# Ordering one kernel's instructions with the scheduler's other machine model

## The chip, the cores and the metric

The kernel is one program on one NeuronCore of a Trainium2 chip. The metric is the time of one execution on the device in microseconds (us). Five engines run side by side, each through its own fixed list of instructions: TensorE (PE; its weight loads are shown apart, as PEld), VectorE (DVE), ScalarE (ACT), GpSimd (POOL) and SyncE (SP), which issues most transfers. An instruction waits for the data that it reads and for the buffer that it writes, and what stands behind it on its engine waits with it.

## The reference

Two transformer-like blocks over 512 tokens of width 1024, batch 1, in float32. The first has an attention layer and a recurrent layer, the second two feed-forward parts around a mixer. Cut to what matters here:

```python
# first block, attention layer: neighbourhood attention (8 heads) and grouped-query attention
y = concat([o_a * silu(ga), o_b * silu(gb)]) @ w_out
# first block, recurrent layer: RWKV state scan in both directions, and a Hyena long convolution
s = s * w_t - sa * b_t + v_t * k_t;  y = s @ r_t           # RWKV, one token
kern = hyena_filters(512, ...)                             # taps, transformed to spectra
z = gate * fft_long_conv(z, kern[:, o], skip[o])           # Hyena, two orders
# second block, mixer: three branches, each with a gate
sol = triangular_solve(a_mat, rhs)                         # gated delta rule, chunks of 64
v_new = u_n - w_n @ state                                  # then 8 chunks in sequence
o = qd_n @ state + qk_n @ v_new
state = state * gl_n + kd_n.T @ v_new
gates = sigmoid(u @ w_branch_gate)                         # 1024 -> 3 x 1024
merged = gates[0] * (o_nsa @ w_nsa) + gates[1] * (o_dn @ w_dn) + gates[2] * (o_mem @ w_mem)
```

## The kernel before

`main()` writes out the whole computation for all five engines in program order, inside a `tile.TileContext`. Tiles come from pools with a number of buffers each, and the context's scheduler decides afterwards in which order the instructions of each engine stand: it plays the program through on a machine model, and at each step an engine takes, of the instructions that the model says could start, the one with the best priority. Priority is program order, moved by `tc.high_priority(...)`. No order is written by hand apart from that.

**Matrix products.** Each large product is split in float32r halves: `wblock` (L96 to L110) loads a weight block `wraw`, ScalarE rounds it to `whi` (L108), VectorE subtracts to get `wlo` (L109), and `mm3` issues three matmuls (L114 to L116): high by high, high by low, low by high. In the rows `mm<-lath,whi` is the input projection of the recurrent layer, `gt<-hh,whi` the gates and other mixer projections, `mm<-whi,oh` the attention layer's output projection. They wait for little but weights, so they can fill TensorE while something else waits.

**Chains.** Four stages have long chains of small steps that go from engine to engine:
- RWKV (`rwkv`, from 760 to 1290 us): six windows of chunks. `unit_inverse` (L1314) inverts triangular blocks: a stream transpose (L1321), 31 pairs of multiply and add on VectorE (L1331, L1333), two stream transposes (L1336, L1337), then 32 by 32 matmuls (L1351, L1353). The steps (`ru` tiles, L1368 to L1429) follow.
- Hyena's spectra (`hy_spectra`): taps (L1575), their squares summed (L1589), products with tables (`fx<-eh,tab0h` and the like), through the pool `fx` with one bank; beside it stands the grouped-query attention (L405, L439, L775).
- DeltaNet (`deltanet`, L2091): per 128 tokens transposes (L2131, L2166) and products (L2177, L2178); one inverse for all heads; then 8 chunks, each of them this loop:

```python
mm(R, T["kbe"], St)                       # L2200, TensorE
Rs = R + vb                               # L2204, VectorE
solve_T(U, TT, Rs)                        # L1368, TensorE
Vs = copy(U)                              # L2207, ScalarE
mm(Q, kd, Vs)                             # L2211, TensorE
St = Q + gl * St                          # L2219, VectorE (L2218 on GpSimd ahead of it)
mm(O, T["qe"], St_old); mm(O, QK, Vs)     # L2223, L2225, TensorE
```
- The mixer's tail: `dn_out` (transposes L2248 of the normalised DeltaNet output), `mem_attn`, `nsa` (L1988) and `merge` with matmuls of 128 columns.

Program order puts `mix_gates` behind `deltanet`, and `RecIn.rest` and `hy_conv` behind the RWKV steps, the last two with a priority part of the way up (`at(x)` in `rwkv`).

## Time and profile before

| | |
|---|---|
| time, median of 3 runs | 2866.03 us (2864.94 to 2867.31) |
| the profiled execution's own time | 2864.4 us |
| its span, first to last instruction | 2861.5 us |
| busy: PE / PEld / DVE / ACT / POOL | 2645.9 / 2125.4 / 1495.3 / 1028.4 / 503.8 us |
| mean granted clock of TensorE | 0.951 of full speed |

The profiled execution lies 1.6 us below the median, and its span 2.9 us below its own time. The granted clock has two levels, 1.0 (2.4 GHz) and 0.5 (1.2 GHz); a figure between them is a mean over a stretch. A pause of TensorE is told with the instruction that ends it and what released that instruction.

### The profile page before, as it was taken

How to read it: one execution, taken by the hardware profiler on the slowest of the kernel's cores; microseconds unless marked ns; L12 is line 12 of the kernel's file. 1: busy time of each engine (PE TensorE's matmuls, PEld its weight loads, DVE VectorE, ACT ScalarE, POOL GpSimd, SP SyncE). 2: the span in 40 equal slices, each digit the busy share in tenths (PEclk: the TensorE clock that was granted, in tenths of full speed). 3: DMA queues.
4: the chain of work that ended last, by engine and by line, in shares of the span. 5: the costliest groups of instructions: out<-in, count | busy, mean ns of one | idle time of the engine just before them, and what ended most of it. 6: DMA issues, size and time to landing. Idle time of an engine off the chain costs nothing.

```text
span 2861.5 us, 43340 instructions
## 1 busy us (share of the span) xinstructions
PE 2645.9 (92%) x16642; PEld 2125.4 (74%) x16642; DVE 1495.3 (52%) x3219; ACT 1028.4 (36%) x2165; POOL 503.8 (18%) x803
## 2 busy tenths in 40 slices
PE   8998998989989889878999998999989999899998
PEld 5897445678767666658888877777868776888887
DVE  4144557736487888685344237762232566444423
ACT  4223335524344444223333224432222663323322
POOL 1011001222343332432000001311010344100000
PEclk9999899989899899988999998999987999999999
DMA  6111431142223332524333323232453315233332
GB/s 231 60 60 55 145 119 63 57 129 81 83 87 113 90 93 66 174 94 138 96 96 96 96 85 108 83 96 91 122 160 104 106 55 161 89 100 100 96 96 88
DMA packets 251018, 290.60 MB, mean 102 GB/s; under 512 B 17415, under 2 KB 197082, under 8 KB 250812
## 3 DMA queue, kind: packets, MB, share of 16 engines
q1 hardware_dynamic: 239292, 251.29, 28.4%
q0 software_dynamic: 10704, 33.41, 3.9%
q8 instruction: 131, 2.15, 0.3%
q10 hardware_dynamic: 816, 3.15, 0.3%
q14 instruction: 75, 0.61, 0.1%
HBM read 247.38 MB, written 35.68 MB: 99 GB/s over the span
## 4 chain that ended last, share of the span: by engine, by line
PE 71%; DVE 11%; issue 5%; POOL 5%; DMA 4%; ACT 3%; SPq 0%; DVEq 0%; POOLq 0%; ACTq 0%
PE mm L114 13%; PE mm L115 13%; PE mm L116 13%; PE gt L114 3%; PE gt L115 3%; PE gt L116 3%; PE ac L116 1%; PE ac L115 1%; PE ac L114 1%; PE ac L874 1%; PE fx L333 1%; PE ac L2053 1%; PE mm L813 1%; DVE wlo L109 1%; PE tr L857 1%
## 5 line engine op out<-in xcount | busy, mean ns | idle before, releaser
L109 DVE TENSOR_TENSOR wlo<-wraw,whi 128x512 fp32r<-128x512 f32 (+1 forms) x390 | 374.5, 961 | 690.1 <-ACT whi L108 683.3
L108 ACT ACTIVATE whi<-wraw 128x512 fp32r<-128x512 f32 (+1 forms) x390 | 323.7, 831 | 792.5 <-PE mm L115 224.3
L114 PE MATMUL mm<-hh,whi 128*128 128x512 f32 (+1 forms) x1024 | 384.0, 376 | 1.0 <-ACT hh L178 0.7
L115 PE MATMUL mm<-hl,whi 128*128 128x512 f32 (+1 forms) x1024 | 383.5, 375 | 0.0
L116 PE MATMUL mm<-hh,wlo 128*128 128x512 f32 (+1 forms) x1024 | 383.0, 374 | 0.1
L114 PEld LDWEIGHTS mm<-hh,whi 128*128 128x128 f32 x1024 | 193.8, 190 | 35.7 <-ACT hh L178 1.3
L116 PEld LDWEIGHTS mm<-hh,wlo 128*128 128x128 f32 x1024 | 193.5, 189 | 35.2 <-DVE wlo L109 1.2
L115 PEld LDWEIGHTS mm<-hl,whi 128*128 128x128 f32 x1024 | 193.9, 189 | 33.1
L114 PE MATMUL mm<-whi,mh 128*128 128x512 f32 (+1 forms) x480 | 172.4, 360 | 1.4 <-DVE th L2270 1.4
L115 PE MATMUL mm<-wlo,mh 128*128 128x512 f32 (+1 forms) x480 | 173.0, 360 | 0.1
L116 PE MATMUL mm<-whi,ml 128*128 128x512 f32 (+1 forms) x480 | 172.7, 360 | 0.0
L114 PE MATMUL gt<-hh,whi 128*128 128x512 f32 (+1 forms) x320 | 128.7, 402 | 7.0 <-ACT whi L108 6.4
L116 PE MATMUL gt<-hh,wlo 128*128 128x512 f32 (+1 forms) x320 | 128.3, 401 | 0.8 <-DVE wlo L109 0.8
L115 PE MATMUL gt<-hl,whi 128*128 128x512 f32 (+1 forms) x320 | 127.6, 399 | 0.0
L283 POOL TENSOR_TENSOR ss<-sq 128x1 f32<-128x1 f32 x8 | 1.6, 201 | 707.3 <-ACT th L277 707.3
L114 PE MATMUL mm<-lath,whi 128*128 128x512 f32 (+1 forms) x280 | 116.4, 417 | 0.1
L116 PE MATMUL mm<-lath,wlo 128*128 128x512 f32 (+1 forms) x280 | 113.7, 407 | 1.0 <-DVE wlo L109 1.0
L115 PE MATMUL mm<-latl,whi 128*128 128x512 f32 (+1 forms) x280 | 113.3, 405 | 0.4 <-DVE latl L179 0.4
L114 PEld LDWEIGHTS mm<-whi,mh 128*128 128x128 f32 x480 | 89.9, 188 | 15.8 <-DVE th L2270 1.8
L115 PEld LDWEIGHTS mm<-wlo,mh 128*128 128x128 f32 x480 | 90.1, 188 | 14.4 <-DVE wlo L109 0.8
L116 PEld LDWEIGHTS mm<-whi,ml 128*128 128x128 f32 x480 | 90.1, 188 | 13.8
L114 PEld LDWEIGHTS gt<-hh,whi 128*128 128x128 f32 x320 | 62.2, 194 | 21.7 <-ACT whi L108 7.4
(732 smaller groups left out, 5987.7 us busy)
## 6 DMA issues: line engine op xcount, KB each, us to landing
wraw<-in_ffn_w_gate SPq DMA_DIRECT2D x44, 512.0 KB, 3.5
wraw<-in_ffn_w_up SPq DMA_DIRECT2D x44, 512.0 KB, 3.6
wraw<-in_ffn_w_down SPq DMA_DIRECT2D x44, 512.0 KB, 3.7
wraw<-in_w_in SPq DMA_DIRECT2D x60, 256.0 KB, 2.8
wraw<-in_rec_w_in SPq DMA_DIRECT2D x58, 256.0 KB, 2.8
wraw<-in_attn_w_in SPq DMA_DIRECT2D x26, 512.0 KB, 3.7
ada_w<-in_rec_ada_w SPq DMA_DIRECT2D x24, 512.0 KB, 3.7
wraw<-in_w_branch_gate SPq DMA_DIRECT2D x48, 256.0 KB, 3.0
```

Source lines behind the costliest of these rows:

```text
L108: nc.scalar.activation(hi, raw, AF.Copy)
L109: self.weng.tensor_sub(lo, raw, hi.bitcast(F32))
L114: mm(out, lh, rh, start=start, stop=False)
L115: mm(out, lh, rl, start=False, stop=False)
L116: mm(out, ll, rh, start=False, stop=stop)
L283: nc.gpsimd.tensor_add(ss, sq[:, i, 0:1], sq[:, i, 1:2])
L333: nc.tensor.matmul(p[o:o + 32], self.cs[:, kk], w[:, k], start=kk < 4, stop=kk >= 4, tile_position=(0, o))
L813: nc.tensor.matmul(ps[p][:, o:o + n], qaT[heads[p], pr, 128 * i:128 * i + 128], ks[p], start=True, stop=True)
L857: nc.tensor.transpose(t[:, j * 128:j * 128 + 128], s[:, a:a + 128], b.ident)
L874: nc.tensor.matmul(o[heads[p], xs], va[rows, n, h * 64:h * 64 + 64], pT[rows, p, j, xs], start=j == 0, stop=j == nk - 1)
L2053: nc.tensor.matmul(o, r["v"][br][:, j], pT[br][:, j].rearrange("p a b -> p (a b)"), start=False, stop=br == 1 and j == i)
```

## The change

One argument of the context is set. The scheduler then plays the program through on its other machine model, which keeps queues and engines in time. No instruction of the computation is added or taken away: TensorE has the same matmuls and DMA queues the same transfers. What differs is the order in which each engine has them, and with it the semaphore waits. TensorE's list has 15,558 lines of difference (10,856 rows before and 11,173 after, where like instructions in a row are one row), VectorE's 5,104.

```diff
-    with tile.TileContext(nc) as tc:
+    with tile.TileContext(nc, schedule_with_timeline_sim=True) as tc:
         main(tc, I, out[0])
```

TensorE at the start of DeltaNet's chunks, before (rows 7350 to 7361; `ac<-Rs,TT` is the solve, `pq<-Vs,kd` the state's product, `ac<-St,Tkbe` the next chunk's first product):

```order
L1368 MATMUL ac<-Rs,TT 64x128 x4
L114 MATMUL gt<-hh,whi 128x512
L115 MATMUL gt<-hl,whi 128x512
L116 MATMUL gt<-hh,wlo 128x512
L114 MATMUL gt<-hh,whi 128x512
L2211 MATMUL pq<-Vs,kd 128x128 x4
L115 MATMUL gt<-hl,whi 128x512
L116 MATMUL gt<-hh,wlo 128x512
L114 MATMUL gt<-hh,whi 128x512
L115 MATMUL gt<-hl,whi 128x512
L2225 MATMUL pq<-Vs,QK 64x128 x4
L2200 MATMUL ac<-St,Tkbe 64x128 x4
```

The same place after the change (rows 7523 to 7533; L2131 is the last transpose of the preparation, L1351 and L1353 the inverse's matmuls):

```order
L2131 MATMUL tr<-ident,dn_16378 128x128
L1351 MATMUL tr<-inv_n,NT 32x32 x32
L1353 MATMUL tr<-TT,inv_x 32x32 x32
L1368 MATMUL ac<-Rs,TT 64x128 x4
L2211 MATMUL pq<-Vs,kd 128x128 x4
L2225 MATMUL pq<-Vs,QK 64x128 x4
L2200 MATMUL ac<-St,Tkbe 64x128 x4
L1368 MATMUL ac<-Rs,TT 64x128 x4
L2211 MATMUL pq<-Vs,kd 128x128 x4
L2223 MATMUL pq<-St,Tqe 64x128 x4
L2225 MATMUL pq<-Vs,QK 64x128 x4
```

Before, some four gate matmuls stand between any two steps of the chain, and 109 rows of them between the last preparation (row 7227) and L1351 (row 7337). After, none stands from the last preparation (row 7523) to row 7562, behind the eighth chunk; the gates' rows stand ahead of it, among the preparation, or from row 7563 on.

TensorE at the fifth of RWKV's six inverses, before (rows 4001 to 4012; `iv` and `mm_10818` are RWKV's own, `mm<-lath` and `mm<-latl` the input projection):

```order
L1351 MATMUL iv<-inv_n,N 32x32 x32
L1198 MATMUL mm_10818<-KR_10792,kT_10795 128x128 x2
L115 MATMUL mm<-latl,whi 128x512
L116 MATMUL mm<-lath,wlo 128x512
L114 MATMUL mm<-lath,whi 128x512
L115 MATMUL mm<-latl,whi 128x512
L116 MATMUL mm<-lath,wlo 128x512
L1353 MATMUL iv<-TT,inv_x 32x32 x32
L1153 MATMUL mm_10846<-lora,wu 128x128 x4
L114 MATMUL mm<-lath,whi 128x512
L115 MATMUL mm<-latl,whi 128x512
L116 MATMUL mm<-lath,wlo 128x512
```

The same inverse after the change (rows 4077 to 4088; L1153 to L1259 are RWKV's preparation of the next window, L1387 the first matmul of a step):

```order
L1198 MATMUL mm_10818<-KR_10792,kT_10795 128x128 x8
L1153 MATMUL mm_10846<-lora,wu 128x128 x4
L1153 MATMUL mm_10878<-lora,wu 128x128 x4
L1351 MATMUL iv<-inv_n,N 32x32 x32
L1219 MATMUL tr<-ident,kT_10870 128x128 x4
L1198 MATMUL mm_10905<-KR_10867,kT_10870 128x128 x8
L1353 MATMUL iv<-TT,inv_x 32x32 x32
L1219 MATMUL tr<-ident,kT_10902 128x128 x4
L1198 MATMUL mm_10925<-KR_10899,kT_10902 128x128 x8
L1259 MATMUL iv<-ident,vw 64x128 x4
L1257 MATMUL iv<-ident,vpad 128x128 x4
L1387 MATMUL ru<-VU_10945,AK 64x64
```

Behind the fourth inverse 208 matmuls of the input projection stand before the change and 9 after it; behind the fifth, 122 before and none after. The rest have moved ahead of it. A third place, in words: behind the last matmul of grouped-query attention (L775) stand no matmuls of Hyena's spectra before the change, and 100 matmul rows after it, a whole last group with L1575 and L1589.

The two feed-forward parts keep their order on TensorE.

## Rows read from the trace of the kernel before

**Rows 1.** The page: span; busy time of each engine; the chain that ended last.
```profile
span 2861.5 us, 43340 instructions
...
PE 2645.9 (92%) x16642; PEld 2125.4 (74%) x16642; DVE 1495.3 (52%) x3219; ACT 1028.4 (36%) x2165; POOL 503.8 (18%) x803
...
PE 71%; DVE 11%; issue 5%; POOL 5%; DMA 4%; ACT 3%; SPq 0%; DVEq 0%; POOLq 0%; ACTq 0%
```

**Rows 2.** Busy time by stretch: from:to length, PE PEld DVE ACT POOL, PEclk, DMA share, GB/s.
```profile
440.00:600.00 160.00, 140.86 (x851) 100.32 (x850) 111.33 (x257) 89.54 (x207) 29.84 (x38) 0.95 0.18 59
760.00:1000.00 240.00, 211.43 (x1931) 165.01 (x1932) 184.39 (x444) 104.77 (x231) 89.42 (x153) 0.88 0.33 96
1000.00:1200.00 200.00, 175.47 (x2189) 131.49 (x2188) 153.31 (x386) 77.67 (x178) 69.20 (x110) 0.97 0.36 112
1330.00:1710.00 380.00, 371.14 (x1759) 311.94 (x1758) 146.81 (x166) 111.68 (x150) 8.72 (x22) 0.99 0.29 90
1800.00:2040.00 240.00, 228.33 (x1396) 176.39 (x1394) 115.76 (x225) 79.92 (x141) 42.95 (x55) 0.99 0.32 96
1920.00:1960.00 40.00, 40.00 (x337) 29.81 (x329) 12.40 (x18) 12.38 (x21) 8.39 (x10) 1.00 0.18 56
2060.00:2200.00 140.00, 122.22 (x582) 105.42 (x581) 38.68 (x68) 26.49 (x51) 16.08 (x27) 0.76 0.47 128
```

**Rows 3.** Groups on VectorE from 1894 to 1919.6: line, operation | busy us, mean ns | idle before.
```profile
L1333 DVE TENSOR_TENSOR inv_x<-inv_x,inv_t 128x126 f32<-128x126 f32 (+22 forms) x31 | 7.9, 256 | 0.9
L1331 DVE TENSOR_TENSOR inv_t<-inv_n,inv_x 128x126 f32<-128x126 f32 (+22 forms) x31 | 7.9, 255 | 0.9
L109 DVE TENSOR_TENSOR wlo<-wraw,whi 128x512 fp32r<-128x512 f32 x9 | 6.1, 682 | 0.0
L1321 DVE STREAM_TRANSPOSE inv_n<-NT 128x1024 f32<-128x1024 f32 x1 | 2.0, 2019 | 0.0
...
L1336 DVE STREAM_TRANSPOSE inv_n<-inv_x 128x512 f32<-128x512 f32 x1 | 1.1, 1061 | 0.0
```

**Rows 4.** Timeline of one DeltaNet chunk: start us, us, engine, line, operation [idle <- releaser].
```profile
1930.13 1.09 PE L2200 MATMUL ac<-St,Tkbe 128*64 128x128 f32 x8
...
1931.26 0.69 DVE L2204 TENSOR_TENSOR Rs<-ac,vb 64x512 f32<-64x512 f32 x1 [2.47 <-PE ac L2200]
...
1932.27 1.08 PE L1368 MATMUL ac<-Rs,TT 64*64 64x128 f32 x8
...
1933.39 0.59 ACT L2207 ACTIVATE Vs<-ac 64x512 f32<-64x512 f32 x1 [2.56 <-PE ac L1368]
...
1934.40 1.16 PE L2211 MATMUL pq<-Vs,kd 64*128 64x128 f32 x8
...
1935.66 0.69 DVE L2219 TENSOR_TENSOR St<-pq,Sg 128x512 f32<-128x512 f32 x1 [0.27 <-PE pq L2211]
...
1936.62 1.09 PE L2223 MATMUL pq<-St,Tqe 128*64 128x128 f32 x8
...
1938.65 1.09 PE L2200 MATMUL ac<-St,Tkbe 128*64 128x128 f32 x8
```

**Rows 5.** TensorE's timeline behind a pause of 12 us.
```profile
1724.53 1.76 PE L166 MATMUL tr<-ident,x 128*128 128x128 f32 x7 [12.02 <-DVE x L157]
```

**Rows 6.** Busy time by stretch behind that pause; columns as in rows 2.
```profile
1730.00:1732.00 2.00, 2.00 (x11) 2.00 (x10) 1.55 (x3) 0.74 (x2) 0.00 (x0) 0.50 0.12 18
1734.00:1736.00 2.00, 2.00 (x19) 1.88 (x19) 1.25 (x2) 1.20 (x2) 0.00 (x0) 1.00 0.00 0
```

**Rows 7.** TensorE's waits from 2060 to 2200: us in total, times, longest.
```profile
PE pq L2248 <- DVE on L2245: 7.1, 3, 4.2
PE gt L114 <- ACT whi L108: 5.5, 1, 5.5
```

**Rows 8.** TensorE's timeline at 607 us.
```profile
607.57 0.80 PE L114 MATMUL mm<-whi,oh 128*128 128x256 f32 x2 [9.13 <-ACT whi L108]
```

**Rows 9.** Line 1589: count, ns min/median/max, first and last start us.
```profile
L1589 PE MATMUL fx<-ones,sq x32: 250/250/370, 480.9 to 577.1; 128*128 128x1 f32 x32
```

## The prediction

> **What bounds the kernel now.** I read the page first: TensorE is busy 2645.9 of 2861.5 us, and the chain that ended last runs through TensorE for 71% of the span [rows 1]. The change takes no work away, so only the other 2861.5 − 2645.9 = 215.6 us can move, together with the matmuls that run at the half clock and are therefore longer. The second view is the table of busy time by stretch [rows 2], to see where those 215.6 us lie. In the first feed-forward stretch (1330 to 1710) TensorE is busy 371.1 of 380 us; its order stays, so nothing changes there. The rest is in four stages:
> - attention beside Hyena's spectra, 440 to 600: 160 − 140.9 = 19.1 us idle, and a pause of 9.13 us behind it [rows 8];
> - RWKV, 760 to 1000: 240 − 211.4 = 28.6 idle, with a mean clock of 0.88; 1000 to 1200: 24.5 idle, with VectorE busy 153.3 of 200;
> - DeltaNet, 1800 to 2040: only 240 − 228.3 = 11.7 idle, and from 1920 to 1960, where its chain of chunks runs, none at all;
> - the mixer's tail, 2060 to 2200: 17.8 idle, at a mean clock of 0.76.
>
> The reader should see that DeltaNet is nearly free now. Its chain is as long as ever, but gate matmuls fill every hole of it. What the order does to that cover decides the forecast.
>
> **The change part by part.** Durations are measured, from the profiled execution before; where the instructions stand comes from the two orders. Nothing here is a time out of the scheduler's own model.
>
> *DeltaNet's inverse.* Before, 109 rows of gate matmuls lie between the last preparation and L1351; afterwards none. What TensorE will then wait for is VectorE's chain: 7.9 + 7.9 us for the 31 pairs, 1.8 idle between them, 2.0 and 1.1 for the stream transposes, 20.7 in all [rows 3]. The nine L109 subtractions that are woven in before (6.1 us) are not counted, since the gates' weights move with the gates. To this come the masking of the last products ahead of it, and a copy behind each of L1351 and L1353; with each such step at the 0.6 to 0.7 us of the copies in [rows 4], and six of them, this is 4. The inverse costs **+25** of idle TensorE.
>
> *DeltaNet's chunks.* Before, a chunk takes 1938.65 − 1930.13 = 8.52 us, and TensorE never stops [rows 4]. Laid bare, the loop is L2200 1.09, Rs 0.04 + 0.69, solve 1.08, Vs 0.04 + 0.59, L2211 1.16, St 0.10 + 0.69, then L2223 and L2225 from 1936.62 to 1938.65, 2.03: together 7.51 us, of which TensorE idles 0.73 + 0.63 + 0.79 = 2.15. Eight chunks make **+17**. The chunk gets shorter, by a microsecond, but the three microseconds of gate matmuls that it carried are now elsewhere, and take time there.
>
> Against these stands the idle time of 1800 to 2040 that is there now, 11.7. Denser gates ahead of the chain can remove most of it; I credit **−8**. DeltaNet nets +34. Its bounds: +42 with nothing credited; and +16, if half of the holes of inverse and chunks (21) is hidden by something that I don't see and 5 of the 11.7 is credited.
>
> *The clock behind the bare stretch.* A pause of 12.02 us is in the trace [rows 5]. Some 6 us after it, TensorE is full but does 11 matmuls in 2 us at a granted clock of 0.50; at 1734 it does 19 at 1.00 [rows 6]. A pause of 25 us ends in the same way, and the work behind it here is the chunk loop, where TensorE has 7.51 − 2.15 = 5.36 us of work in 7.51. I take **+6**: the first chunk or so at half clock, 5.36 each. Lower bound 0; upper bound all eight chunks, 8 × 5.36 = 43.
>
> The Trainium skill, in "TensorE: Matmul & The Clock Gate", section "HAM oscillation — how this bites in real kernels", says that a loop whose matmul bursts alternate with waits can be throttled again at each wait and so stay slow. Here the row shows a single recovery after one pause, and no row shows such a loop at either clock; by the row the sum has +6, by the page it would have up to +43. This is the third rival below.
>
> *RWKV.* The input projection is used up early: 208 of its matmuls stand behind the fourth inverse before, 9 after; behind the fifth 122 and none. One takes about 371.1 / 1759 = 0.21 us (the mean of the feed-forward stretch [rows 2], whose matmuls are of the same kind). So 122 × 0.21 = 26 us of cover is missing where the last two inverses and the steps run, and 199 × 0.21 = 42 us stands earlier, where there are 28.6 us of idle time to fill. Both happen. If VectorE's chain is what the stage waits for throughout (it is busy 77% of it), the early filling gains nothing, because the fill then delays the steps, and the late holes cost. I take **+7**, between −42 (all of the moved work goes into idle time and slow clock, and the tail is set by VectorE anyway) and +26. It is nearer to the middle than to either end because the two amounts are of a size.
>
> *Spectra beside attention.* A whole last group of spectra now runs behind the last attention matmul. Between the four L1589 groups lie (577.1 − 480.9) / 3 = 32 us each, with attention woven in [rows 9]; alone a group has some 96 table matmuls, and if they run at half of the 0.21 us, since they have half of the columns, 10 us of work. Its holes are then at most 32 − 10 = 22. Against it, the 9.13 us pause, which waits for the first output weights [rows 8], can shrink behind a later start of that product, and attention without spectra has its part of the 19.1. I take **+5**, between −9 and +22.
>
> *The mixer's tail.* Here the order may help. Its 17.8 us of idle time contain 7.1 of L2248 waiting for VectorE and 5.5 of gates waiting for `whi` [rows 7]; afterwards L2248's transposes are spread among matmuls. The clock of 0.76 over 140 us means that about 0.24 / 0.5 × 140 = 67 us were at half; without the 17.8 idle, that is 49 us of work that would take 25 at full clock. At most 17.8 + 25 = 43 can be won, and at least nothing, since the same matmuls of 128 columns come again behind the same kind of waits. I take **−20**, half.
>
> The sum: 34 + 6 + 7 + 5 − 20 = +32. Made against the profiled execution, 2864.4 + 32 = 2896.4, whose own time lies 1.6 us below the median; the forecast is 2898 us. TensorE's weight loads, GpSimd and the DMA queues are put at nothing: the transfers are the same, and a dense run of fills asks for weights no faster than the feed-forward stretch, which keeps TensorE full with a DMA share of 0.29 [rows 2]. Without that cover the known price is one more pause like the 9.13 us [rows 8].
>
> **The rivals.**
> - *Faster: RWKV's early filling pays in full.* One mechanism: 42 us of input projection falls into the 28.6 us of idle time and the half clock of 760 to 1000 (0.88 means 0.12 / 0.5 × 240 = 58 us at half), and VectorE's chain is not delayed by it. Then the RWKV term is about −40 instead of +7, and the time 2898 − 47 = 2851; with a tail that wins its whole 43 as well, 2828. For it speaks that the idle time is really there; against it, that VectorE is busy 77% there and steps now stand behind fills in TensorE's list. It decides when the stage from 760 us gets shorter by more than 26 us plus what the tail wins less than 20.
> - *Nothing: the same.* All terms cancel and TensorE's 2645.9 us of work decide: 2866. For it: 92% busy. Against it: DeltaNet's 42 us of holes have no row that fills them.
> - *Much slower: the clock stays at half* through the chunk loop (+43 instead of +6) and the tail wins nothing: 2898 + 37 + 20 = 2955; with only the first, 2935. For it: the clock of 0.76 in the tail, where waits are shorter than the inverse. Against it: the recovery in [rows 6].
>
> **How the numbers follow.** A difference of 0.2% (5.7 us) is about what a measurement of this kernel can tell from none. Likeliest, the sum: 0.55, with its own range of 2878 to 2922. The faster rival: 0.23. Nothing: 0.08, a quarter of it on either side of the 0.2%. The half clock: 0.14. So faster is 0.23 + 0.02 = 0.25, the same 0.04 + 0.02 from the sum's low edge = 0.06, slower 0.69. The range: 2842 leaves out the lower half of the faster rival, 0.12, and 2945 half of the slow one, 0.07; together nearly 2 in 10.
>
> **What would show it.** In the changed profile: the gap before L1351 near 25 us, with VectorE's L1331 and L1333 back to back beneath it; the chunks with a period near 7.5 us, and TensorE busy some 70% of it; a clock row of 0.5 for 5 to 10 us behind the gap; DeltaNet's gates dense at 1.00 ahead of it. RWKV from its fourth inverse on without `mm<-lath` rows, and pauses before L1351; a shorter, denser start of it. The stretch with L2248 without its 7.1 us of waits. The forecast is wrong if TensorE's idle total does not rise by some 30 us, if the gap before L1351 is filled by anything, or if the stage of RWKV comes out shorter than its 530 us.

## The result and the profile after

The changed kernel takes 2902.31 us (median of 4 runs, 2895.59 to 2905.38); on the same chip the kernel before takes 2865.49 (4 runs, 2851.37 to 2867.31). The ratio is 1.0136, with a 95% interval of 1.0098 to 1.0174: slower by 1.4%. The forecast was 2898. Two executions of the experiments below took more than twice the time of all others (6403.99 us of e6_rwkv_hold, its profiled one, and 11739.58 us of e10_spread) and are left out.

The profiled execution took 2905.38 us. Its page, three lines that answer to [rows 1]:

```profile
span 2903.6 us, 43396 instructions
...
PE 2659.3 (92%) x16642; PEld 2168.4 (75%) x16642; DVE 1514.4 (52%) x3219; ACT 1022.6 (35%) x2165; POOL 501.3 (17%) x803
...
PE 49%; DVE 5%; DMA 2%; issue 2%; ACT 2%; POOL 1%; SPq 0%; DVEq 0%; POOLq 0%; ACTq 0%
```

The span grew by 42.1 us, and TensorE's busy time by 13.4 with the same 16,642 matmuls: part of them ran longer. Where that is, the start times of milestones tell (us from the span's start, read from the two timelines):

| first matmul of | before | after | difference |
|---|---|---|---|
| attention's output projection | 607.6 | 610.1 | +2.5 |
| the recurrent layer's input projection | 687.8 | 692.6 | +4.8 |
| the first feed-forward part | 1347.3 | 1347.6 | +0.3 |
| the mixer | 1724.5 | 1726.1 | +1.6 |
| the inverse in DeltaNet (L1351) | 1919.5 | 2007.9 | +88.4 |
| the second feed-forward part | 2488.0 | 2528.1 | +40.1 |

So RWKV, spectra and attention together come out even, and the mixer has the loss. (Most of the +88.4 is work that now comes earlier, the gates; the loss is what is left of it behind the mixer.) Cut at the start of DeltaNet, at its inverse (L1351) and at the end of its loop, the mixer has four stretches; the third, from L1351 on, is called the loop here. This is busy time by stretch of the kernel before, columns as in [rows 2]:

```profile
1724.50:1810.20 85.70, 83.62 (x403) 68.03 (x403) 62.69 (x92) 39.22 (x64) 13.84 (x13) 0.95 0.32 88
1810.20:1919.50 109.30, 98.84 (x568) 75.66 (x567) 76.04 (x167) 40.69 (x73) 28.65 (x38) 0.98 0.30 90
1919.50:1987.80 68.30, 68.23 (x524) 51.05 (x524) 19.81 (x28) 18.66 (x31) 10.49 (x12) 1.00 0.17 50
1987.80:2488.00 500.20, 464.13 (x2552) 386.25 (x2551) 229.76 (x609) 195.91 (x503) 122.31 (x200) 0.92 0.41 120
```

And this is the changed kernel: the same four stretches, then the gap ahead of L1351, the stretches of RWKV, and the first feed-forward part, which keeps its row.

```profile
1726.10:1818.00 91.90, 86.95 (x415) 70.64 (x416) 66.21 (x96) 39.45 (x67) 11.49 (x18) 0.94 0.30 85
1818.00:2007.90 189.90, 165.99 (x921) 135.64 (x922) 93.18 (x190) 62.73 (x109) 27.96 (x38) 0.94 0.36 106
2007.90:2101.60 93.70, 74.88 (x424) 62.29 (x424) 13.50 (x19) 10.68 (x18) 10.01 (x12) 0.51 0.00 1
2101.60:2528.10 426.50, 394.45 (x2289) 335.35 (x2289) 214.16 (x592) 180.50 (x476) 123.12 (x196) 0.95 0.42 125
...
1984.70:2007.90 23.20, 0.20 (x4) 0.07 (x4) 20.87 (x70) 0.00 (x0) 0.78 (x2) 0.54 0.00 0
...
760.00:1000.00 240.00, 227.48 (x1954) 178.50 (x1953) 204.83 (x450) 113.43 (x248) 98.60 (x163) 0.94 0.40 119
1000.00:1200.00 200.00, 164.26 (x2076) 132.19 (x2076) 159.05 (x393) 69.20 (x164) 72.07 (x113) 0.81 0.28 90
1330.00:1710.00 380.00, 371.97 (x1758) 312.99 (x1757) 145.23 (x164) 109.44 (x145) 6.94 (x17) 0.99 0.29 90
```

Idle time is the first number less the second. Up to the inverse it went from 109.30 − 98.84 = 10.5 to 23.9 us, of which 23.0 are the gap; in the loop from 0.1 to 18.8; behind it from 36.1 to 32.1. The loop has 424 matmuls now where it had 524: the gates are gone from it. Yet it takes 93.7 us instead of 68.3, and its granted clock is 0.51. Beneath the gap VectorE works back to back through the inverse; its groups, as in [rows 3]:

```profile
L1333 DVE TENSOR_TENSOR inv_x<-inv_x,inv_t 128x126 f32<-128x126 f32 (+22 forms) x31 | 7.9, 256 | 1.1
L1331 DVE TENSOR_TENSOR inv_t<-inv_n,inv_x 128x126 f32<-128x126 f32 (+22 forms) x31 | 7.9, 256 | 1.1
L1321 DVE STREAM_TRANSPOSE inv_n<-NT 128x1024 f32<-128x1024 f32 x1 | 1.9, 1887 | 0.0
```

The timeline of the gap's end and of one chunk, as in [rows 4]:

```profile
2007.86 1.92 PE L1351 MATMUL tr<-inv_n,NT 32*32 32x32 f32 x64 [23.00 <-issue]
...
2021.30 1.97 PE L2200 MATMUL ac<-St,Tkbe 128*64 128x128 f32 x8
...
2023.30 0.69 DVE L2204 TENSOR_TENSOR Rs<-ac,vb 64x512 f32<-64x512 f32 x1 [3.95 <-PE ac L2200]
...
2024.14 1.93 PE L1368 MATMUL ac<-Rs,TT 64*64 64x128 f32 x8 [0.88 <-DVE Rs L2204]
2026.11 0.59 ACT L2207 ACTIVATE Vs<-ac 64x512 f32<-64x512 f32 x1 [4.12 <-PE ac L1368]
...
2026.76 2.07 PE L2211 MATMUL pq<-Vs,kd 64*128 64x128 f32 x8 [0.68 <-ACT Vs L2207]
2028.94 0.69 DVE L2219 TENSOR_TENSOR St<-pq,Sg 128x512 f32<-128x512 f32 x1 [4.94 <-PE pq L2211]
...
2029.68 1.97 PE L2223 MATMUL pq<-St,Tqe 128*64 128x128 f32 x8 [0.85 <-DVE St L2219]
...
2033.48 0.90 PE L2200 MATMUL ac<-St,Tkbe 128*64 128x128 f32 x3
```

The small steps on VectorE and ScalarE take as long as before (0.69, 0.59, 0.69), and the three waits 0.88, 0.68 and 0.85. What has nearly doubled is each of the matmul groups: L2200 1.09 to 1.97, L1368 1.08 to 1.93, L2211 1.16 to 2.07. The period is 2033.48 − 2021.30 = 12.18 us, where the bare chunk had been worked out to 7.51, and it is 12.0 to 12.4 for all chunks. The clock had fallen before the loop began: it is 0.99 up to the gap and 0.54 in the gap, whose row stands above.

### The profile page after: what moved, and what is told of

Same layout as the page of the kernel before. It is cut to its first block, busy times and chain, and to the rows that moved or that the text cites. A ratio compares the mean times of both kernels' runs of the same rounds, so it can differ in the third digit from the quotient of the medians.

```text
span 2903.6 us, 43396 instructions
## 1 busy us (share of the span) xinstructions
PE 2659.3 (92%) x16642; PEld 2168.4 (75%) x16642; DVE 1514.4 (52%) x3219; ACT 1022.6 (35%) x2165; POOL 501.3 (17%) x803
## 3 DMA queue, kind: packets, MB, share of 16 engines
q8 instruction: 131, 2.15, 0.3%
## 4 chain that ended last, share of the span: by engine, by line
PE 49%; DVE 5%; DMA 2%; issue 2%; ACT 2%; POOL 1%; SPq 0%; DVEq 0%; POOLq 0%; ACTq 0%
PE mm L114 10%; PE mm L115 10%; PE mm L116 10%; PE gt L114 4%; PE gt L115 4%; PE gt L116 3%; PE ac L2053 1%; DMA oraw<-d_od 1%; PE ac L1368 1%; PE pq L2211 1%; PE pq L2225 0%; PE mm L2026 0%; PE mm L1946 0%; PE pq L2223 0%; PE ac L2200 0%
## 5 line engine op out<-in xcount | busy, mean ns | idle before, releaser
L109 DVE TENSOR_TENSOR wlo<-wraw,whi 128x512 fp32r<-128x512 f32 (+1 forms) x390 | 373.6, 959 | 686.4 <-ACT whi L108 664.0
L116 PE MATMUL mm<-hh,wlo 128*128 128x512 f32 (+1 forms) x1024 | 369.1, 375 | 0.2 <-DVE wlo L109 0.2
L114 PE MATMUL mm<-whi,mh 128*128 128x512 f32 (+1 forms) x480 | 153.0, 360 | 3.0 <-DVE th L2270 3.0
L125 POOL TENSOR_SCALAR rstd<-ss 128x1 f32<-128x1 f32 (+2 forms) x60 | 19.1, 319 | 330.2 <-DVE ss L694 205.7
```

The source lines that it names most:

```text
L109: self.weng.tensor_sub(lo, raw, hi.bitcast(F32))
L114: mm(out, lh, rh, start=start, stop=False)
L116: mm(out, ll, rh, start=False, stop=stop)
L125: nc.gpsimd.tensor_scalar(r, ss, q / n, q * eps, op0=OP.mult, op1=OP.add)
```

## The experiments

Line numbers in an experiment's rows can be some lines off, by what was inserted. Several kernels hold gate blocks back. They do it with a one-column copy on GpSimd from a tile of the chain into the raw weight tile ahead of its load, so that the load, and with it the block's matmuls, can't come before that step (e1_held12 uses one tile for all loads):

```diff
 # wblock
+        if getattr(self, "after", None):
+            nc.gpsimd.tensor_copy(raw[:, 0, 0:1], self.after.pop(0))
```

The theory was that the loss is DeltaNet's lost cover: idle time, and a half clock behind it. The rivals were that the clock falls for the gap alone, and that it falls for the loop's own short waits. Each ratio below is against runs of the kernel before on the same chip; it is not the quotient of two medians.

### What the bare loop costs, without the changed scheduler

`e4_gates_first` is the kernel before, scheduler and all; only the call that makes the gates is moved ahead of DeltaNet in program order, so that nothing fills DeltaNet.

```diff
+        mix_gates(b, I, uh, ul, gd, gp, "gt")
...
-        mix_gates(b, I, uh, ul, gd, gp, "gt")
```

> The kernel before, on the old machine model, with one call moved: the gates stand ahead of DeltaNet in the program and so have priority over it. Its order has no gate matmul under the inverse or in the chunk loop, as in the changed kernel, while the rest of the kernel keeps the old order. Theory A (the lost cover is what costs): a pause of about 23 us before L1351, chunks of about 12 us at half clock, and a time of 2866 + 23 + 19 + 35 less the 10 us of preparation's idle time that go, so 2920 to 2935 us, or from 2900 if the mixer's tail gains what it gained in the changed kernel. Theory B (it is the other differences of the new order): 2866, within 10 us.

Measured: 2974.54 us, ratio 1.0395 [1.0349, 1.0441]. Busy time from the preparation's start to the inverse, and of the loop, and TensorE's three longest waits there:

```profile
1945.10:2054.40 109.30, 53.16 (x357) 40.85 (x356) 57.55 (x135) 20.85 (x36) 26.70 (x38) 0.65 0.05 15
2054.40:2149.00 94.60, 75.92 (x424) 63.16 (x424) 13.63 (x20) 10.68 (x18) 9.99 (x12) 0.50 0.00 1
```

```profile
PE tr L1351 <- issue: 22.8, 1, 22.8
PE tr L2166 <- DVE yk L2148: 12.9, 4, 3.8
PE tr L2166 <- DVE yq L2148: 10.4, 3, 4.1
```

The gap of 23 us and the loop of 94 us at half clock are thus properties of DeltaNet without filling, whichever scheduler laid it bare. The loss is larger than the changed kernel's, because here the preparation has no filling either: 56.1 us idle up to the inverse, gap included, where the kernel before has 10.5 and the changed one 23.9, and a clock of 0.65. The expectation, 2920 to 2935, had credited the preparation with a gain of 10 us instead, and was too low.

### Which waits lower the clock

`e2_warm_inv` puts 24 matmuls that nothing needs (128 by 512, into a spare bank) under the inverse of the changed kernel; `e3_warm_both` puts three more beside each chunk's waits. Neither changes what is computed.

```diff
 # e2 and e3, ahead of the inverse
+    for _ in range(24):
+        mm(junk, b.ident, QK.rearrange("p i h t -> p (i h t)")[:, 512:1024], start=True, stop=True)
 # e3 alone, in each chunk
+            mm(junk, b.ident, St.rearrange("p h d -> p (h d)"), start=True, stop=True)
+        mm(junk, b.ident[hr], Rs[hr], start=True, stop=True)
+            mm(junk, b.ident[hr], Vs[hr], start=True, stop=True)
```

> The changed kernel plus 24 float32 matmuls of 128 by 512 on a spare bank, whose result nobody reads, between the last masked product and the inverse's first matmul. They do no work that is needed, so the wait stays as long as it is and only TensorE's clock can gain. Theory A1 (the pause of 23 us lowers the clock, and the chunk loop by itself keeps it up, once it is up): chunks of 7.5 us instead of 12.1, so about 8 x 4.6 = 37 us less: 2865 us. Theory A2 (the loop's own waits of 0.7 to 0.85 us lower it again): the loop begins at full clock and falls back to 12 us a chunk after one or two: 2890 to 2900 us. Theory B (the clock has nothing to do with it): 2902.

> As the run before, plus three such unneeded matmuls in every chunk, one in each of its three waits. If a float32 matmul of 128 by 512 takes about 0.9 us at full clock, a chunk is 7.5 to 8.2 us at full clock. Theory A1 or A2: the whole loop at a granted clock of 1.0 and the time 2866 to 2875 us; if the run before stays near 2900, the difference between the two is the price of the loop's own short waits. Theory B: above 2902, because the added matmuls only lengthen the chunks.

Measured: 2895.5 us, ratio 1.0117 [1.0078, 1.0156], and 2873.98 us, ratio 1.0041 [1.0016, 1.0066]. First e2's inverse and loop, with the loop's beginning apart, then e3's loop, whole and in two parts:

```profile
1983.00:2006.10 23.10, 20.96 (x49) 9.04 (x48) 20.77 (x70) 0.00 (x0) 0.77 (x2) 1.00 0.00 1
2006.10:2097.90 91.80, 72.91 (x424) 60.55 (x424) 13.56 (x19) 10.69 (x18) 9.99 (x12) 0.54 0.00 1
...
2006.10:2010.00 3.90, 2.37 (x128) 2.21 (x128) 1.91 (x2) 0.59 (x1) 1.03 (x2) 1.00 0.00 0
2010.20:2018.20 8.00, 5.92 (x25) 4.93 (x25) 1.38 (x2) 1.06 (x2) 1.21 (x2) 0.50 0.00 0
```

```profile
1997.40:2067.30 69.90, 66.40 (x467) 44.00 (x466) 13.53 (x19) 10.69 (x18) 9.99 (x12) 0.90 0.00 1
...
2000.80:2014.40 13.60, 12.15 (x76) 8.24 (x68) 2.08 (x3) 1.77 (x3) 1.25 (x2) 0.50 0.01 1
2014.40:2067.30 52.90, 52.32 (x303) 34.08 (x302) 9.57 (x14) 8.33 (x14) 7.70 (x8) 1.00 0.00 1
```

With the gap filled the clock is 1.00 through it and through L1351 and L1353. It falls right behind these, ahead of the first chunk, and the loop still spends 91.8 us, nearly all at half. In e3 the clock falls at the same place, but it is back at 1.00 from 2014.4 on and stays there: the loop takes 69.9 us, although it does more matmuls. So the gap isn't needed for the slow loop, although in the changed kernel the clock does fall in it. What decides in the loop is whether its own waits of 0.7 to 0.9 us, three in each chunk, are filled. Leaving them bare costs 91.8 − 69.9 = 21.9 us of the loop in clock and idle time, and 21.5 by the medians; the unneeded matmuls take time too, so this is the least that it costs. One rival is left: the filling puts large matmuls where waits were, so no run tells the waits apart from the small size of the loop's own matmuls. Both expectations held (2890 to 2900 for e2 by its theory A2, 2866 to 2875 for e3). Unneeded matmuls win back most of the loss, but they take the time in which the gates could have run.

### Putting the gates back

`e1_held12` holds the last 12 of the 24 gate blocks until the masked products ahead of the inverse are there.

```diff
+    n = 12 * 128
+    gemm_T(b, I["w_branch_gate"], 0, n, uh, ul, [(0, 512, tag)], ev, step=128)
+    b.after = b.dn_last
+    gemm_T(b, I["w_branch_gate"], n, 3 * D - n, uh, ul, [(0, 512, tag)], lambda j, ps: ev(j + 12, ps), step=128)
...
+    b.dn_last = QK[:, 3, 3, 63:64]
```

> The changed kernel, with the weight loads of the last 12 of the 24 gate blocks held back until DeltaNet's last mask product is there (a one-column copy into the raw tile from the masked products, on GpSimd, ahead of each load). Nothing of the computation is left out. By its order 120 gate matmuls stand under the inverse, 14 to 27 in each hole of the first four chunks and none in the last four. Theory A (the loss is DeltaNet's lost cover): the pause of 23.0 us before L1351 shrinks below 2 us, the first chunks run at full clock, and the time falls by 23 for the pause, about half of the loop's 18.8 us of idle time, and 17 to 35 for the clock: 2835 to 2853 us. Theory B (the clock is low there for another reason, or the time is set elsewhere): within 10 us of 2902. Theory C (holding the gates back only moves the hole into the preparation): 2890 to 2902, with new pauses ahead of L2177.

Measured: 2886.7 us, ratio 1.0091 [1.0059, 1.0123], between theory A (2835 to 2853) and theory C (2890 to 2902). The gap is gone, with 120 gate matmuls under the inverse. But the scheduler puts 14 to 27 matmuls into each hole of the first chunks, for holes of 0.7 to 0.9 us: up to 24 of the gates at 0.23 us each, then 25 to 27 of half the width at 0.12, so 3.2 to 5.6 us of work. The chunk periods are 19.74, 16.06 and 12.51, then these are used up and the loop is bare. Busy time around that point:

```profile
2026.00:2034.00 8.00, 7.93 (x62) 6.99 (x62) 2.38 (x3) 1.86 (x3) 1.05 (x1) 1.00 0.26 68
2034.00:2042.00 8.00, 5.69 (x45) 4.54 (x42) 1.37 (x2) 1.18 (x2) 1.05 (x1) 1.00 0.12 33
2042.00:2050.00 8.00, 5.62 (x35) 4.58 (x35) 1.39 (x2) 1.18 (x2) 1.05 (x1) 0.87 0.00 0
2050.00:2060.00 10.00, 7.63 (x33) 6.21 (x32) 1.37 (x2) 1.18 (x2) 0.00 (x0) 0.50 0.00 0
```

Here one can watch the clock fall: the first bare chunk runs at 1.00 (its period is 7.67 us, near the 7.51 that was worked out), and the last at 0.50 (12.17), with no long pause between them. Meanwhile the preparation misses the held blocks: up to the inverse TensorE is idle for 31.5 us although the gap is gone; in the changed kernel it was 23.9, of which the gap 23.0.

This is also what the change does on TensorE: with its other model, the scheduler puts more into each hole, and so uses the gates up before the inverse. In the changed kernel's trace the full holes of the preparation have 14 to 36 gate matmuls each, before the change mostly 3 to 15. Why that model does so is not shown here. The next four kernels give it smaller pieces, each released by a step of the chain.

```diff
 # e5_paced: 16 blocks free, 8 half blocks at the inverse, then one half block with each chunk
+    b.after = [b.dn_rel[0]] * 8 + [b.dn_rel[1 + c] for c in range(8) for _ in range(1)]
 # e5c_fine: in place of the last, quarter pieces, released by Rs, Vs and St in turn
+    b.after, b.qmax = [b.dn_rel[1 + k * 23 // 32] for k in range(32)], 1
 # e10_spread: 2 blocks free, 9 in pieces along the preparation, 5 at the inverse, 4 in the loop, 4 behind
+    gates(2, [])
+    gates(9, [b.dn_prep[max(0, k * n // 36 - 0)] for k in range(36)], 2)
+    gates(5, [b.dn_prep[-1]] * 10)
+    gates(4, [b.dn_rel[1 + k * 23 // 32] for k in range(32)], 1)
+    gates(4, [b.dn_rel[-1]] * 8)
 # e10_spread_b: 8 in smaller pieces, 6 at the inverse
+    gates(8, [b.dn_prep[max(0, k * n // 64 - 0)] for k in range(64)], 1)
+    gates(6, [b.dn_prep[-1]] * 12)
```

> The changed kernel with the weight loads of the last 8 of the 24 gate blocks held back: 8 half blocks until the last masked product, and one half block more for each chunk of the loop (a one-column copy on GpSimd ahead of each load). Nothing is left out. By its order 96 gate matmuls stand under the inverse and 12 in one hole of each chunk; the other two holes of a chunk stay bare. Theory A (lost cover, paid as idle time and as clock): the pause before L1351 goes (23 us), chunks take 7.5 + 12 x 0.23 - 0.73 = 9.6 us at full clock instead of 12.1 and carry 2.8 us of gates each, so 20 + 22 us; some 15 come back as holes in the preparation: 2850 us. Theory A with the clock still falling (two bare holes a chunk are enough for that): 2875 to 2885. Theory C (held gates only move the hole into the preparation, as they did in part with 12 blocks): 2885 to 2900.

> As the run before, but the last 4 gate blocks are loaded in quarter blocks of 3 matmuls, each released by a step of a chunk, so that every hole of the loop gets 1 to 6 gate matmuls, as before the change. Theory A: chunks near 8.5 us at full clock and 2840 to 2850 us, not above the run before. If the run before keeps full clock too, the two are within 5 us; if there the clock falls, this one is 20 to 30 us below it. Against it stand 32 more small splits on ScalarE and VectorE, at most 0.3 us each.

> The changed kernel with the 24 gate blocks paced through the whole of DeltaNet: 2 free, 9 in half-size pieces of 6 matmuls that are released one after another by the steps of the preparation, 5 at the preparation's end, 4 in pieces of 3 by the steps of the chunks, 4 behind the loop. By its order the holes of the preparation have 6 to 18 gate matmuls (14 to 36 in the changed kernel, 4 to 15 before it), 141 stand under the inverse, and 1 to 6 in each hole of the loop. Nothing is left out. Theory A (the loss is that the new model puts too many fills into each hole, and runs out of them): the preparation has some 12 us of idle time, the inverse none, the chunks 8.5 us at full clock, and the tail keeps its gain: 2840 to 2855 us, 5 to 20 below the kernel before on the same chip. Theory C (there are too few gates for all holes, so that the holes only move): no better than the run with fine pacing, 2880 to 2890. Theory D (the tail's gain was bought by the early gates and goes with them): as the kernel before, within 5 us.

> As the run before, with other shares: 8 blocks through the preparation in pieces of 3 matmuls, 6 at its end; by its order 3 to 17 gate matmuls in a hole of the preparation and 122 under the inverse, and the first steps behind the inverse carry 22 each. Theory A: within 6 us of the run before, as the holes are covered in both; more small splits on ScalarE and VectorE cost up to 5 us. If it is more than 10 us slower, the small splits on VectorE, which stand in its list between the preparation's steps, are what costs.

| kernel | median us | ratio to before, 95% | loop's chunk periods, us |
|---|---|---|---|
| e5_paced | 2900.79 | 1.0118 [1.0049, 1.0187] | 12.36, 9.74, 11.59, 12.64 ... |
| e5c_fine | 2884.59 | 1.0070 [1.0041, 1.0100] | 10.82, 8.85, 8.53, 9.49 ... |
| e10_spread | 2883.45 | 1.0047 [1.0015, 1.0079] | 11.31, 8.82, 8.54, 9.23 ... |
| e10_spread_b | 2876.42 | 1.0023 [0.9994, 1.0051] | 9.96, 9.73, 8.40, 9.22 ... |

A half block per chunk (e5_paced) is still too coarse: its loop has a clock of 0.81, and nothing is won. In quarters (e5c_fine) the loop, from 1989.2 on, has 0.91 in the mean and 1.00 from 2005.8 on, and the idle time is in the preparation instead: 24.6 us up to the inverse. Spread over the whole of DeltaNet in pieces of 6 and then 3 matmuls, most of the loss is gone, and e10_spread_b can't be told from the kernel before; its median is 12.8 us above that kernel's on its chip (2863.61), within the interval. The first three did not come out as theory A had it (2840 to 2855): e5_paced is just above all that was expected, e5c_fine 35 us above, e10_spread lies where theory C put it (2880 to 2890, the holes only move), and e10_spread_b is 7.0 below e10_spread, where at most 6 had been expected either way. The preparation and loop of e10_spread_b:

```profile
1808.80:1944.30 135.50, 114.20 (x585) 81.83 (x584) 81.82 (x213) 50.32 (x122) 44.18 (x136) 0.92 0.26 79
1944.30:2024.50 80.20, 78.76 (x561) 59.09 (x560) 26.11 (x52) 24.45 (x58) 19.56 (x67) 0.98 0.16 49
```

What it still lacks is in the preparation (21.3 us idle, before 10.5), and in a wait of 8.89 us of the last held gates for their weights, behind the loop.

### RWKV

`e6_rwkv_hold` holds the last 16 loads of the input projection in the changed kernel until RWKV's triangular blocks 4, 5 and 6 are there; `e6c_rwkv` holds them earlier and in a smaller dose; `e7_both` is e5c_fine and e6_rwkv_hold together.

```diff
+                    if turn == 6:          # e6_rwkv_hold, e7_both
+                        b.after = [b.rw_rel[i] for i, n in ((3, 3), (4, 6), (5, 7)) for _ in range(n)]
                     # e6c_rwkv: ((2, 2), (3, 7), (4, 5), (5, 2))
```

> The changed kernel, with the last 16 weight loads of the recurrent layer's input projection held back until the fourth, fifth and sixth triangular blocks of RWKV are there. By its order 156 of its matmuls stand behind the fourth inverse and 62 behind the fifth, against 9 and 9 in the changed kernel and 208 and 122 before it. DeltaNet is left as changed. The term of the prediction under test is RWKV's: +7 us between -42 and +26. If late cover is worth its work (62 to 156 matmuls of 0.21 us, and the half clock from 1080 to 1160), the time falls by 10 to 30 us: 2872 to 2892. If the early filling is worth as much, the two cancel: within 6 us of 2902.

> The changed kernel with the last 16 weight loads of the input projection held back by the third to the sixth triangular blocks: 84 of its matmuls stand behind the fourth inverse and 8 behind the fifth (9 and 9 in the changed kernel, 208 and 122 before). The earlier run of this kind had medians near 2900 to 2914, so I expect no gain: within 8 us of 2902. A fall of 15 us or more would say that the late cover is worth more than the early filling; a rise of as much, the reverse.

> The fine pacing of DeltaNet's gates and the held input projection together. If the two terms are independent, their gains add: 2902 less 55 less 10 to 20, so 2827 to 2845 us, below the kernel before by 20 us or more. If the time of the whole is set elsewhere (the transfers, or the attention stage), it is not below the better of the two.

Measured: e6_rwkv_hold 2913.52 us, 1.0133 [1.0059, 1.0208] (three runs, no rows); e6c_rwkv 2891.58, 1.0085 [1.0057, 1.0113]; e7_both 2891.49, 1.0094 [1.0067, 1.0121], which is no better than e5c_fine alone and far from the 2827 to 2845 of added gains. The larger dose wins nothing, even with 156 of the projection's matmuls back behind the fourth inverse and 62 behind the fifth (the changed kernel has 9 and none; the expectation's second 9 is a slip). The smaller one lies 10.7 us below the changed kernel by medians, more than the 8 expected, but the two intervals overlap, and its stretch from 1000 to 1200 is idle for 43.6 us, more than the changed kernel's 35.7:

```profile
1000.00:1200.00 200.00, 156.44 (x2078) 123.72 (x2077) 164.44 (x396) 68.04 (x160) 73.26 (x122) 0.86 0.31 98
```

The whole recurrent layer can be compared as well, from the first matmul of its input projection to the first of the feed-forward part. Seven of the other traces (e1, e2, e3, both e5 and both e10) have the changed kernel's order on TensorE up to there, but for at most four places, so with its own there are eight: 640.6 to 654.9 us, 647.9 in the mean. e6c_rwkv, e7_both and e11_all, with the hold, take 644.6, 650.1 and 643.1, inside that range. The kernel before and e4_gates_first, whose order there is the same, take 659.5 and 661.9 (the latter on the chip of e1, e2 and e3, which take 644.4 to 649.7).

So RWKV isn't where the loss is, as the milestones had said, and what e6c wins isn't shown to come from there. On the contrary, the new order makes that layer shorter in all eight traces, by 13 us in the mean; against it, the input projection begins 7 us later (693.4 in the mean, before 687.8 and 684.5).

### All of it together

`e11_all` is e10_spread_b with e6c's hold, and with the last four gate blocks released five steps before the loop's end instead of at it.

```diff
-    gates(4, [b.dn_rel[-1]] * 8)
+    gates(4, [b.dn_rel[-5]] * 8)
+                        b.after = [b.rw_rel[i] for i, n in ((2, 2), (3, 7), (4, 5), (5, 2)) for _ in range(n)]
```

> The finest pacing of the gates so far (the second spreading through all of DeltaNet, 2876 us) with two edits more: the last four gate blocks are released by the loop's fifth step from its end instead of by its end, so that their weights are not waited for behind it (8.89 us for whi there), and the last input-projection loads are held for RWKV's triangular block in the smaller dose (10 us below the changed kernel). Theory (the changed model's loss is only where its fillings go): both gains add, 2876 - 9 - 10 = about 2857, at or just below the kernel before. Rival (fillings held in one place are missed in another, and the first block takes its own back): not additive, 2870 or more.

Measured: 2867.82 us (12 runs; before 2861.94 on the same chip), ratio 1.0014 [0.9997, 1.0031]: no different from the kernel before, and the nearest to it. It lies 8.6 us below e10_spread_b by medians, between the two theories' numbers, though by the ratios only 0.0009, within both intervals. One half of the expectation failed outright: the wait behind the loop is still there. The timeline of SyncE's queue, of the weights that are waited for, and of TensorE; then SyncE's wait:

```profile
2025.32 2.04 SPq L1964 DMA_DIRECT2D w<-in_cmp_w_k  x4
2027.47 2.07 SPq L104 DMA_DIRECT2D wraw<-in_w_branch_gate  x3
...
2035.17 0.31 ACT L110 ACTIVATE whi<-wraw 128x128 fp32r<-128x128 f32 x1 [9.25 <-DMA wraw<-in_w_branch_gate]
...
2035.53 0.80 PE L116 MATMUL gt<-hh,whi 128*128 128x512 f32 x1 [9.35 <-ACT whi L110]
```

```profile
SPq L1964 <- PE pq L2259: 3.8, 1, 3.8
```

The gates' loads stand on SyncE behind four other loads, L1964, and these wait for L2259, the loop's last product. So they are issued at 2027.47, after the loop's end, however early they are released, and land 7.7 us later. The release was not what they waited for.

## Why the prediction was right in its sum, and where it was wrong

The direction, the place and the two largest items of idle time were right. That the sum came out well is luck: a large term that was too low met others that were too high. The profiled span grew by 42.1 us, against +32 predicted. The table is of one execution before and one after:

| step | predicted | measured |
|---|---|---|
| DeltaNet's inverse | +25 | +23.0 |
| idle time of the chunks | +17 | +18.8 |
| preparation, credited | −8 | −9.6 |
| clock behind the bare stretch | +6 | +36.7 |
| RWKV | +7 | −4.5 |
| spectra and attention | +5 | +4.8 |
| the mixer's tail | −20 | −20.4 |
| not foreseen | 0 | −7 |

**The inverse** is VectorE's chain, as said: 7.9 + 7.9 + 1.9 and a last transpose, without a gate's L109 between them, and TensorE does nothing beneath it. **The chunks** idle by 18.8 us over eight, 2.35 each where 2.15 was worked out. **The preparation's** gates are dense: 23.9 − 23.0 = 0.9 us of idle time is left of 10.5.

**The clock** is the step that failed. It was put at "the first chunk or so at half clock, 5.36 each", because after one pause [rows 6] shows the clock back at 1.00 within some 10 us. That row has dense matmuls behind its pause; the chunk loop has not. In the loop 73.5 of the busy 74.9 us ran at 0.50 (counted over its matmuls, by the clock's records in the trace), which costs half of that, 36.7. e1_held12 bears it out with the same chunk at either clock: 12.17 − 7.67 = 4.5 us more, 36 for eight. So the first half of the third rival, the chunk loop at half clock, happened, at the 0.14 that it was given; its second half, a tail that wins nothing, did not. Its price for the first half alone, 2935, was missed because other terms came out lower, RWKV's most of all. The rule of the Trainium skill, "TensorE: Matmul & The Clock Gate", section "HAM oscillation — how this bites in real kernels", that a loop whose matmul bursts alternate with waits can be throttled again at each wait, was the better guide here than the row. The Trainium skill's case, however, has waits longer than the work between them, and a clock that goes to and fro; here the waits are 0.7 to 0.9 us, shorter than each of the matmul groups between them, and the clock fell once and stayed. The prediction also gave the gap as the cause. With the gap filled, e2_warm_inv kept the slow loop, and with the loop's waits filled too, e3_warm_both did not: what the loop has in its own waits decides, not the gap.

**RWKV.** Both amounts that the step weighed are in the rows. From 760 to 1000 idle time fell from 28.6 to 12.5 us and the clock rose from 0.88 to 0.94; from 1000 to 1200 idle time rose from 24.5 to 35.7 and the clock fell from 0.97 to 0.81 [rows 2]. They nearly cancel in this pair, with −4.5 left, the smallest gain of the eight traces above: by their mean it is −13. The early filling won more than the late holes cost, so the term had the wrong sign. The pauses came in other places than the one named: ahead of the fifth L1351 there is one of 0.2 us. **The spectra** and attention cost what was said, where +4.8 is all that lies ahead of the input projection, though the pause at the output projection didn't shrink (9.02 us, before 9.13 [rows 8]).

**The tail.** The waits of L2248, and of the gates for `whi` [rows 7], are gone from the list of waits, as foreseen. These made 12.6 us, but the idle time behind the loop fell by 4.0 only, as others came in their place; the busy time that ran at the half clock went from 67.0 to 34.3 us, worth 16.4: together 20.4. That this meets the −20 so closely is luck, for it was half of an upper bound, and for 140 us of the 500.

**Not foreseen** are −7 us: +2.9 of idle time at the mixer's start, +0.5 of clock, and +3.3 outside the mixer, most of it behind the last matmul, on one side; on the other −13.3 of busy time in the mixer that neither gaps nor the clock account for. TensorE's busy time in the four stretches rises by 722.3 − 714.8 = 7.5, while the clock alone would have made it 36.7 + 0.5 − 16.4 = 20.8. A part may be the price of weaving: before, a chunk took 8.52 us with 12 gate matmuls of 0.23, which leaves 5.7 for its own, where the bare one has 5.36; that is an estimate of some 3 us over eight chunks. The rest stays open.

Of the signs that the prediction named, the gap came, the dense gates ahead of it (TensorE busy 165.8 of 166.7 us, at 0.99) and the idle total, from 215.6 to 244.3 us. The chunks' period of 7.5 and the short row at half clock did not. And one of its three signs of being wrong came: a shorter recurrent layer.

That the loss is where the gates lie is shown by the experiments from two sides: e4_gates_first makes it with the old scheduler, and e10_spread_b undoes most of it under the new one. The new order is better than the old in the recurrent layer, by the eight traces, and in the mixer's tail, by one pair of executions. No run turns that into a gain of the whole: the best version of it equals the kernel before.

## What to carry to other kernels

Before an order is changed, look for the chains that it now fills and work out two prices for laying one bare: its idle time, and as much again as the loop's matmul time at full clock, because a loop of short dependent steps may run at the half clock from end to end (here 4.5 us more for 5.4 us of matmuls a chunk). A filling is a stock to be spread: a chain wants pieces of the size of its holes, each released by a step of the chain, and a scheduler that fills a hole of 0.8 us with 4 us of work is as bad for the rest of the chain as one that fills none. If a piece's load waits, look at what stands ahead of it on the issuing queue before moving its release.

## What was unexpected of the hardware

The bare chunk loop, whose waits are 0.7 to 0.9 us, fell from a granted clock of 1.00 to 0.50 without any longer pause (e1_held12: 1.00, 0.87, 0.50 in successive rows), and in the changed kernel it did not come back (0.51 over 93.7 us). The same loop with its holes filled with unneeded matmuls had 0.90, with gates in small pieces 0.98 (e10_spread_b), and before the change 1.00. In e3_warm_both the clock had fallen ahead of the first chunk, and came back to 1.00 within the second. The matmuls that keep the clock up need not be useful: three unneeded ones per chunk made the loop 21.9 us shorter.
